# A two-layer diffusion backbone: second halves of the first scale and shift by high and low parts, constant products first, head reordered

## Chip, cores and metric

The kernel runs on one core of one Trainium2 chip. The metric is device time in microseconds (us), the median of several runs. TensorE multiplies matrices; VectorE (DVE), ScalarE (ACT) and GpSimd (POOL) work elementwise; SyncE (SP) issues most loads. Each engine executes its own instructions strictly in the order in which they were written for it, and semaphores make it wait for others.

## What is computed

Two layers over 256 latent tokens and 256 context tokens of width 1024, float32. Cut to what matters here, layer 0 begins so:

```python
mod_l = (silu(c) @ w_ada + b_ada)            # c: conditioning vector, w_ada: (1024, 6*1024)
mod_c = silu(c_ctx) @ w_ada + b_ada
sh1, sc1, g1, sh2, sc2, g2 = split(mod, 6)   # for latent and context
hl = xl * (1 + sc1_l) + sh1_l                # "h": the modulated input
hc = xc * (1 + sc1_c) + sh1_c
pl = hl @ w_in ; pc = hc @ w_in              # the wide input projection
# token mixers: Hyena long conv, attention, pooling; gates; output projection; layer norm; SwiGLU
# Hyena's filter: h = sin(freq*(feats@w1+b1)); h = sin(freq*(h@w2+b2)); h @ w3, times a window
```

So the first scale and shift (`sc1`, `sh1`) must be known before any token can be projected. They are two matrix-vector products: 1024x1024 weights each, against the two vectors `c` and `c_ctx`.

## The kernel before

A float32 product is made with the faster type `float32r` and three products: each operand is split into a high part (ScalarE, a copy to float32r, `L162`) and a low part (VectorE or GpSimd, the difference, `L159`), and `mm3` (`L169` to `L171`) sums high·high, high·low and low·high. Weights stream in blocks of 128x1024: `wfetch` loads `raw`, makes `whi` and `wlo` (or `wx`, for the first ones). A dense unit is 24 products (8 slices of the width, 3 each) with 512 columns (256 latent, 256 context tokens); its result is named `u`, `uv`, `ux` and so on.

The head of the program (`run`) does this:

- `ccol`, the two conditioning vectors, gets its silu (tanh on ScalarE, the rest on VectorE).
- `ada_raw(j, half)` loads half of the weights of shift (`j` 0) or scale (`j` 1): four tiles `adar` of 512 KB. "Half" is half of the 1024 output columns, so the first half modulates slices 0 to 3 of `h`, the second half slices 4 to 7. `ada_half` multiplies them in plain float32 with the two columns of `ccol` as the stationary operand (`L1220`, eight products of 512 columns), copies the row out (`adarow`, ScalarE), turns it into columns by four small transposes (`adat`, TensorE), and adds the bias (`mod`, VectorE).
- `first_h(x, h, half)` makes four slices of `h`, high part on ScalarE (`hh`), low part on VectorE and GpSimd (`hf`, `hl`).
- `early_half` runs the part of the first three dense units (`u`) that needs only the first half of `h`; the second half follows in the function `dense`.
- Hyena's filter is a background generator: a small product `L337`, a sine (`L309` to `L315`: VectorE brings the argument into range, ScalarE takes `Sin`), a small product `L343`, a second sine, a cast `hfh`, and then, per quarter, the weights `wfh` (`L398`) and the products `L406` and `L407`. `pump()` lets it take its next step, so the calls of `pump` set where its instructions stand.
- The rows of `silu` (`csg`, `L1179`) are for later adaLN weights.

Nothing decides at run time. The tile framework orders the instructions of each engine when the program is built; `with self.tc.high_priority(n)` moves a block ahead of others in that order. Tiles of one tag rotate through a fixed number of buffers (`bufs`), and a new one waits until the old one's readers are done. After the head, TensorE runs one dense unit after another to the end.

Of the kernel before, what the change touches and what calls it, by code (L numbers as in the profile page):

```python
# [11 lines left out]
F32R = mybir.dt.float32r  # L12
I32 = mybir.dt.int32
AF = mybir.ActivationFunctionType
ALU = mybir.AluOpType
# [3 lines left out]
P = 128  # L19
D = 1024  # L20
KT = D // P
# [31 lines left out]
V_CW, V_CB, V_BADA, V_QG, V_KG, V_HYD = 40, 112, 136, 184, 185, 186  # L53
NV = 194
# [11 lines left out]
class Kernel:  # L66
# [868 lines left out]
    def fold(self, g, b, sc, sh):  # L935

        nc = self.nc
        f = self.small([P, 2, KT], "fold", tag="fold", bufs=8)
        nc.vector.tensor_tensor(out=f[:, 0], in0=g, in1=sc, op=ALU.mult)
        nc.vector.tensor_tensor(out=f[:, 1], in0=b, in1=sc, op=ALU.mult)  # L940
        nc.vector.tensor_tensor(out=f[:, 1], in0=f[:, 1], in1=sh, op=ALU.add)
        return f[:, 0], f[:, 1]

    def scaled(self, g, b):
        f = self.small([P, 2, KT], "alp", tag="fold", bufs=8)
# [179 lines left out]
    def run(self):  # L1125
        nc = self.nc
        cc = self.const([P, KT, 2], "ccol")
        nc.scalar.dma_start(out=cc, in_=self.c_col)
        self.vecs = self.const([P, DEPTH, NV + 6], "vecs")
        self.ones = self.const([P, P], "ones")  # L1130
        nc.vector.memset(self.ones, 1.0 / D)
        self.ident = self.const([P, P], "ident")
        make_identity(nc, self.ident)
        self.mod = [[self.const([P, 2, KT], f"mod{l}{j}") for j in range(6)] for l in range(DEPTH)]
        th = self.const([P, KT, 2], "ccolt")
        nc.scalar.activation(th, cc, AF.Tanh, scale=0.5)
        nc.vector.tensor_scalar(out=th, in0=th, scalar1=0.5, scalar2=0.5, op0=ALU.mult, op1=ALU.add)
        nc.vector.tensor_tensor(out=cc, in0=cc, in1=th, op=ALU.mult)
        x = self.big(F32, [P, KT, 512], name="x")
        h = self.pair(512, "h")  # L1140
        self.start_filters(0)
        self.start(itertools.chain(self.filter_hidden(0), self.filter_chain(0)))
        raws = [self.ada_raw(1, 0), self.ada_raw(0, 0)]
        nc.scalar.dma_start(out=self.vecs[:, :, :NV], in_=self.vecs_d)
        nc.sync.dma_start(out=x[:, 0:4], in_=self.x_t[:, 0:4])
        for j, raw in zip((1, 0), raws):
            with self.tc.high_priority(200):
                self.ada_half(cc, j, 0, raw)
            self.pump()
        self.first_h(x, h, 0)  # L1150

        wx = self.big(F32R, [P, 2, 2, D], name="wx")
        for i in range(2):
            self.wfetch((wx[:, i, 0], wx[:, i, 1]))
        raws = self.ada_raw(1, 1)
        self.wfetch(None, nc.gpsimd)
        self.early = [(self.wq.popleft(), self.mm(name="u")) for _ in range(3)]
        self.early_half(h, *self.early[0], 0)
        for j in (1, 0):
            with self.tc.high_priority(1000):  # L1160
                self.ada_half(cc, j, 1, raws)
            if j:
                raws = self.ada_raw(0, 1)
                for k in (4, 6):
                    nc.sync.dma_start(out=x[:, k : k + 2], in_=self.x_t[:, k : k + 2])
                for w, o in self.early[1:]:
                    self.early_half(h, w, o, 0)
# [37 lines left out]
    def ada_raw(self, j, half):  # L1205

        raws = []
        for kp in range(4):
            raw = self.t4(shape=[P, 2, 512], name="adar")
            self.nc.sync.dma_start(out=raw, in_=self.ada0[j, half * 4 + kp])  # L1210
            raws.append(raw)
        return raws

    def ada_half(self, cc, j, half, raws):

        nc = self.nc
        o = self.aux(name="adar")
        for kp in range(4):
            for k in range(2):
                nc.tensor.matmul(o[:2], lhsT=cc[:, 2 * kp + k], rhs=raws[kp][:, k], start=kp + k == 0, stop=kp + k == 4)  # L1220
        row = self.t2(name="adarow")
        nc.scalar.activation(row[:2], o[:2], AF.Copy)
        tp = self.aux([P, 4, 2], name="adat")
        for m in range(4):
            nc.tensor.transpose(tp[:, m], row[:2, m * P : (m + 1) * P], self.ident[:2, :2])
        c = 4 * half
        for s in range(2):
            nc.vector.scalar_tensor_tensor(out=self.mod[0][j][:, s, c : c + 4], in0=tp[:, :, s], scalar=float(j),
                                           in1=self.v(0, V_BADA + 8 * j + c, 4), op0=ALU.add, op1=ALU.add)

# [126 lines left out]
```

## Time and profile before

| | us |
|---|---|
| runs | 1717.17, 1719.15, 1722.42; median 1719.15 |
| the profiled execution | 1716.89 |
| its span, first to last instruction | 1715.1 |
| TensorE busy in the span | 1662.9 (97%) |
| VectorE busy | 1218.8 (71%) |
| ScalarE busy | 709.1 (41%) |
| GpSimd busy | 224.6 (13%) |
| first matmul of the scale and shift | 6.38 |
| first matmul of the fourth dense unit (`uv`) | 57.86 |

Times in the trace count from the span's start; 1.8 us of the execution lie around the span. A share of busy time is an average over stages: this change touches the first 60 us alone, and what it is worth is read from who waits for whom there.

### The profile page before, as it was taken

The page shows a single profiled execution, that of the slowest core. Times are in us where ns is not written, and L with a number is a line of the kernel's source. Part 1 is how long each engine was busy: PE and PEld are TensorE (multiplying, and loading weights), DVE is VectorE, ACT ScalarE, POOL GpSimd, SP SyncE. Part 2 cuts the span into 40 slices and gives each one's busy share as a digit, 9 for nine tenths or more (in the row PEclk, how much of TensorE's full clock was granted, in tenths as well). Part 3 has the DMA queues.
Part 4 walks back from the last instruction along what each step waited for, and adds up shares of the span by engine and source line. Part 5 has one row for each costly group of instructions (what it writes and reads, how often), then busy time and mean ns, then how long its engine had stood idle before and what let it go on. Part 6 is the DMA issues. An engine that isn't in the chain of part 4 may idle for free.

```text
span 1715.1 us, 25592 instructions
## 1 busy us (share of the span) xinstructions
PE 1662.9 (97%) x9926; PEld 1448.2 (84%) x9926; DVE 1218.8 (71%) x2124; ACT 709.1 (41%) x1130; POOL 224.6 (13%) x232
## 2 busy tenths in 40 slices
PE   8999999999999999999999999998899999999996
PEld 1888888888888888988888877898899999989996
DVE  3777778755677775788876566498866696796655
ACT  3533432534454433542222222264435564564442
POOL 1134541000210000000000011124510210000000
PEclk9999999999999999999999999999999999999998
DMA  8422222553422344226666654244336525645552
GB/s 322 149 87 87 62 87 75 153 158 125 135 74 90 113 160 130 98 91 196 193 201 191 210 177 148 62 149 131 115 108 194 172 89 161 196 140 190 182 186 89
DMA packets 68898, 243.35 MB, mean 142 GB/s; under 512 B 8166, under 2 KB 8744, under 8 KB 68520
## 3 DMA queue, kind: packets, MB, share of 16 engines
q1 hardware_dynamic: 67192, 236.78, 43.3%
q0 software_dynamic: 1168, 4.72, 0.9%
q8 instruction: 78, 1.28, 0.3%
q14 instruction: 44, 0.36, 0.1%
q10 hardware_dynamic: 416, 0.21, 0.1%
HBM read 238.01 MB, written 1.05 MB: 139 GB/s over the span
## 4 chain that ended last, share of the span: by engine, by line
PE 82%; DVE 11%; ACT 2%; issue 2%; POOL 1%; DMA 1%; ACTq 0%; DVEq 0%; POOLq 0%
PE f L169 6%; PE f L171 6%; PE f L170 6%; PE b L169 4%; PE g L169 4%; PE g L171 4%; PE g L170 4%; PE b L171 4%; PE b L170 4%; PE w L169 4%; PE w L171 4%; PE w L170 4%; DVE wlo L159 2%; PE ux L169 2%; PE ux L171 2%
## 5 line engine op out<-in xcount | busy, mean ns | idle before, releaser
L162 ACT ACTIVATE whi<-raw 128x1024 fp32r<-128x1024 f32 x322 | 340.7, 1059 | 710.9 <-issue 210.4
L159 DVE TENSOR_TENSOR wlo<-raw,whi 128x1024 fp32r<-128x1024 f32 x311 | 397.8, 1280 | 216.0 <-ACT whi L162 214.0
L190 DVE SCALAR_TENSOR_TENSOR junk<-ada,silu 128x1024 bf16<-128x1024 f32 x128 | 158.7, 1241 | 38.6 <-DMA ada<-adat 38.0
L169 PE MATMUL f<-h2h,whi 128*128 128x512 f32 (+1 forms) x320 | 125.1, 391 | 0.1
L170 PE MATMUL f<-h2l,whi 128*128 128x512 f32 (+1 forms) x320 | 124.5, 389 | 0.0
L171 PE MATMUL f<-h2h,wlo 128*128 128x512 f32 (+1 forms) x320 | 124.5, 389 | 0.0
L169 PE MATMUL w<-a,whi 128*128 128x256 f32 (+1 forms) x284 | 90.3, 318 | 0.0
L169 PE MATMUL f<-h,whi 128*128 128x256 f32 x312 | 88.4, 283 | 1.9 <-DVE fraw L930 1.9
L170 PE MATMUL w<-a,whi 128*128 128x256 f32 (+1 forms) x284 | 89.2, 314 | 0.0
L171 PE MATMUL w<-a,wlo 128*128 128x256 f32 (+1 forms) x284 | 89.2, 314 | 0.0
L171 PE MATMUL f<-h,wlo 128*128 128x256 f32 x312 | 87.6, 281 | 0.6 <-DVE wlo L159 0.6
L170 PE MATMUL f<-h,whi 128*128 128x256 f32 x312 | 88.1, 283 | 0.0
L169 PE MATMUL g<-hh,whi 128*128 128x512 f32 x192 | 75.6, 394 | 0.0
L171 PE MATMUL g<-hh,wlo 128*128 128x512 f32 x192 | 75.4, 392 | 0.0
L170 PE MATMUL g<-hl,whi 128*128 128x512 f32 x192 | 75.3, 392 | 0.0
L169 PEld LDWEIGHTS f<-h2h,whi 128*128 128x128 f32 x320 | 60.0, 188 | 14.1 <-DVE sg L973 0.9
L171 PEld LDWEIGHTS f<-h2h,wlo 128*128 128x128 f32 x320 | 60.1, 188 | 13.6
L170 PEld LDWEIGHTS f<-h2l,whi 128*128 128x128 f32 x320 | 60.1, 188 | 13.1
L169 PEld LDWEIGHTS f<-h,whi 128*128 128x128 f32 x312 | 58.4, 187 | 2.4 <-issue 2.3
L171 PEld LDWEIGHTS f<-h,wlo 128*128 128x128 f32 x312 | 59.3, 190 | 0.8 <-DVE wlo L159 0.8
L170 PEld LDWEIGHTS f<-h,whi 128*128 128x128 f32 x312 | 58.6, 188 | 0.0
L169 PEld LDWEIGHTS w<-a,whi 128*128 128x128 f32 x284 | 53.4, 188 | 4.1 <-issue 0.2
(474 smaller groups left out, 4802.0 us busy)
## 6 DMA issues: line engine op xcount, KB each, us to landing
raw<-wst SPq DMA_DIRECT2D x336, 512.0 KB, 3.5
ada<-adat SPq DMA_DIRECT2D x80, 512.0 KB, 3.8
adar<-ada SPq DMA_DIRECT2D x16, 512.0 KB, 10.2
qsw<-q POOLq DMA_DIRECT2D x16, 128.0 KB, 5.2
x<-x_t POOLq DMA_DIRECT2D x1, 2048.0 KB, 9.6
x<-x_t SPq DMA_DIRECT2D x1, 1024.0 KB, 10.6
x<-x_t SPq DMA_DIRECT2D x2, 512.0 KB, 10.2
silu<-c_row SPq DMA_DIRECT2D x2, 512.0 KB, 7.5
```

The costliest lines, as they stand in the source:

```text
L159: (eng or self.nc.vector).tensor_tensor(out=lo, in0=src, in1=hi.bitcast(F32), op=ALU.subtract)
L162: self.nc.scalar.activation(hi, src, AF.Copy)
L169: t.matmul(out, lhsT=ah, rhs=bh, start=start, stop=False)
L170: t.matmul(out, lhsT=ah, rhs=bl, start=False, stop=False)
L171: t.matmul(out, lhsT=al, rhs=bh, start=False, stop=stop)
L190: nc.vector.scalar_tensor_tensor(out=junk, in0=raw, scalar=1.0, in1=self.silu[:, s], op0=ALU.mult, op1=ALU.mult, accum_out=mod[:, s, m : m ...
```

## The change

1. Twelve products of the constant tile `ones` with itself are written ahead of all other work of TensorE; nobody reads their result.
2. The first halves of scale and shift are multiplied as before, but both groups directly one after the other (class `Ada`, `passes`), and each is turned into columns afterwards (`columns`).
3. The second halves (`half == 1`) are no longer plain float32: `ccol` is split into four columns `ccolp` (two high, two low), each of the eight weight tiles is split into high (`ahi`, ScalarE, in buffers of the tags `whi` and `wlo`) and low (`alo`, VectorE, in two buffers of the tag `big`), and 16 products per group give four rows, which the product with `fold4` turns into columns and adds up.
4. The head is reordered: the scale's second half comes ahead of the first half of `h`; the tables of the long convolution (`start_filters`, `dft_tables`) come later; the third weight's low part is made by VectorE and no longer by GpSimd; the filter's steps come at other calls of `pump`.
5. `fold` and `alp` rotate through 7 buffers where there were 8; `ccolt` is a tile of the tag `t2`.

```diff
-        f = self.small([P, 2, KT], "fold", tag="fold", bufs=8)
+        f = self.small([P, 2, KT], "fold", tag="fold", bufs=7)
...
+        o = self.aux(name="warm")
+        for _ in range(12):
+            nc.tensor.matmul(o[:, :P], lhsT=self.ones, rhs=self.ones, start=True, stop=True)
...
+        cp = self.sb.tile([P, KT, 4], F32R, tag="ccolp", name="ccolp", bufs=1)
+        self.split(cp[:, :, 0:2], cp[:, :, 2:4], cc)
+        self.fold4 = self.vecs[:4, 0, NV : NV + 2]
+        nc.vector.tensor_tensor(out=self.fold4, in0=self.ident[:4, 0:2], in1=self.ident[:4, 2:4], op=ALU.add)
...
-        self.start_filters(0)
         self.start(itertools.chain(self.filter_hidden(0), self.filter_chain(0)))
-        raws = [self.ada_raw(1, 0), self.ada_raw(0, 0)]
+        first = [Ada(self, cc, 1, 0), Ada(self, cc, 0, 0)]
...
-        for j, raw in zip((1, 0), raws):
-            with self.tc.high_priority(200):
-                self.ada_half(cc, j, 0, raw)
-            self.pump()
+        with self.tc.high_priority(1000):
+            first[0].passes(0, 4)
+            first[1].passes(0, 4)
+            first[0].columns()
+        self.pump()
+        scale = Ada(self, cc, 1, 1)
+        with self.tc.high_priority(1000):
+            scale.passes(0, 1)
+            first[1].columns()
+
+        wx = self.big(F32R, [P, 2, 2, D], name="wx")
+        self.wfetch((wx[:, 0, 0], wx[:, 0, 1]))
+        with self.tc.high_priority(1000):
+            scale.passes(1, 4)
+            scale.columns()
         self.first_h(x, h, 0)
...
+        self.wfetch((wx[:, 1, 0], wx[:, 1, 1]))
+        shift = Ada(self, cc, 0, 1)
+        self.early = [(self.wq.popleft(), self.mm(name="u")) for _ in range(2)]
+        for w, o in self.early:
+            self.early_half(h, w, o, 0)
+        with self.tc.high_priority(500):
+            shift.passes(0, 4)
+            shift.columns()
+        for k in (4, 6):
+            nc.sync.dma_start(out=x[:, k : k + 2], in_=self.x_t[:, k : k + 2])
+        with self.tc.high_priority(1000):
+            self.wfetch()
+        self.early.append((self.wq.popleft(), self.mm(name="u")))
+        self.early_half(h, *self.early[2], 0)
+        self.start_filters(0)
         self.dft_tables(0)
-        with self.tc.high_priority(50):
+        with self.tc.high_priority(1000):
             self.first_h(x, h, 1)
+        self.pump()
...
+class Ada:
...
+    def passes(self, a, b):
+        k = self.k
+        self.o = self.o or k.aux(name="adar")
+        for kp in range(a, b):
+            ws = [self.raws[kp]]
+            if self.parts:
+                tag = ("whi", "wlo")[kp % 2]
+                ws = [k.sb.tile([P, 2, 512], F32R, tag=tag, name=k.nm("ahi"), bufs=3), self.los[:, kp]]
+                k.split(*ws, self.raws[kp])
+            for i in range(2):
+                for m, w in enumerate(ws):
+                    k.nc.tensor.matmul(self.o[: self.n], lhsT=self.cc[:, 2 * kp + i], rhs=w[:, i],
+                                       start=kp + i + m == 0, stop=kp + i == 4 and m == len(ws) - 1)
```

The order that this gives differs from that of before in the head alone. Three places of it follow. The first is ScalarE's queue around the filter's first sine (`hf1h`; `adarow` are the rows of scale and shift, `ahi` the high parts of the scale's second half). Before:

```order
L1222 ACTIVATE adarow_123<-adar_114 2x512
L315 ACT_TABLE_LOAD
L315 ACTIVATE hf1h_134<-sa_135 64x256
L1222 ACTIVATE adarow_154<-adar_145 2x512
L1195 ACTIVATE hh_88<-x_87,mod_71,mod_72 128x256 x7
L315 ACTIVATE hf2h_165<-sa_166 128x256
```

The same place after the change:

```order
L1260 ACTIVATE adarow_147<-adar_129 2x512
L162 ACTIVATE ahi_179<-adar_169 128x1024
L162 ACTIVATE ahi_200<-adar_171 128x1024
L315 ACT_TABLE_LOAD
L315 ACTIVATE hf1h_158<-sa_159 64x256
L1260 ACTIVATE adarow_186<-adar_138 2x512
L162 ACTIVATE ahi_207<-adar_173 128x1024
L162 ACTIVATE ahi_214<-adar_175 128x1024
L162 ACTIVATE wx_195<-raw_196 128x1024
```

Two high parts stand ahead of the sine now; behind it stand the shift's row (`adarow_186`), the other two high parts and the first weight. The second sine (`hf2h`) has left this place.

The second place is VectorE's queue around the argument of that second sine (`sa_166`, `sa_402`). Before, it stands between the shift's first half (`mod_71`) and the first half of `h`:

```order
L1228 SCALAR_TENSOR_TENSOR mod_71<-adat_156,vecs 128x4 x2
L309 TENSOR_SCALAR sa_166<-hf_25_163,hfs_92 128x256
L310 TENSOR_SCALAR sn_167<-sa_166 128x256
L311 TENSOR_SCALAR sn_167<-sn_167 128x256
L313 SCALAR_TENSOR_TENSOR sa_166<-sn_167,sa_166 128x256 x3
L314 TENSOR_SCALAR sa_166<-sa_166 128x256
L1197 TENSOR_SCALAR hf_180<-x_87,mod_72,mod_71 128x256
```

After the change it stands at the end of the second half of `h` (`hl_106` is its last low part; `hyb` is a table, `wlo_424` a weight):

```order
L159 TENSOR_TENSOR hl_106<-hf_392,hh_105 128x256
L309 TENSOR_SCALAR sa_402<-hf_77_399,hfs_107 128x256
L159 TENSOR_TENSOR hyb_360<-dftraw_363,hyb_360 128x512
L310 TENSOR_SCALAR sn_403<-sa_402 128x256
L159 TENSOR_TENSOR wlo_424<-raw_421,whi_423 128x1024
L311 TENSOR_SCALAR sn_403<-sn_403 128x256
L313 SCALAR_TENSOR_TENSOR sa_402<-sn_403,sa_402 128x256 x3
L314 TENSOR_SCALAR sa_402<-sa_402 128x256
L1198 SCALAR_TENSOR_TENSOR silu<-csg_430,silu 128x512
```

It moved from before the first low part of `h` to behind the last one.

The third place is TensorE's queue at the filter's first quarter (`hf` with `wfh` and `hfh`). Before, it stands behind the dense unit `uv`:

```order
L169 MATMUL uv_451<-hh_88,whi_358 128x512
L170 MATMUL uv_451<-hl_89,whi_358 128x512
L171 MATMUL uv_451<-hh_88,wlo_359 128x512
L406 MATMUL hf_91_476<-wfh_438,hfh_176 128x256
L407 MATMUL hf_91_476<-wfl_439,hfh_176 128x256
```

After the change two of its eight products stand ahead of `uv`, behind the last of the units `u`:

```order
L170 MATMUL u_347<-hl_106,whi_343 128x512
L171 MATMUL u_347<-hh_105,wlo_344 128x512
L406 MATMUL hf_103_535<-wfh_497,hfh_412 128x256
L406 MATMUL hf_104_541<-wfh_497,hfh_412 128x256
L169 MATMUL uv_510<-hh_105,whi_417 128x512
```

They moved ahead by one dense unit, and with them the wait for `wfh` and `hfh`.

## Rows read from the trace of the kernel before

**Rows 1.** The page, busy time: us, share of the span, instructions.

```profile
PE 1662.9 (97%) x9926; PEld 1448.2 (84%) x9926; DVE 1218.8 (71%) x2124; ACT 709.1 (41%) x1130; POOL 224.6 (13%) x232
```

**Rows 2.** Timeline of TensorE: start, length, instruction, count, [idle before <- releaser].

```profile
6.38 8.96 PE L1220 MATMUL adar<-adar,ccol 128*2 128x512 f32 x16 [6.38 <-DVE ccol L1138]
16.11 0.38 PE L1225 MATMUL adat<-ident,adarow 2*128 2x2 f32 x4 [0.77 <-ACT adarow L1222]
16.41 0.64 PE L337 MATMUL hf<-feats,hfs 33*64 33x256 f32 x2
16.99 7.03 PE L1220 MATMUL adar<-adar,ccol 128*2 128x512 f32 x16
...
34.73 7.03 PE L1220 MATMUL adar<-adar,ccol 128*2 128x512 f32 x16
...
42.81 0.41 PE L1225 MATMUL adat<-ident,adarow 2*128 2x2 f32 x4
...
57.86 0.40 PE L169 MATMUL uv<-hh,whi 128*128 128x512 f32 x1
58.09 0.39 PE L170 MATMUL uv<-hl,whi 128*128 128x512 f32 x1
```

**Rows 3.** Timeline of VectorE.

```profile
17.10 0.54 DVE L309 TENSOR_SCALAR sa<-hf,hfs 64x256 f32<-64x256 f32 x1 [0.34 <-PE hf L337]
...
18.30 1.32 DVE L313 SCALAR_TENSOR_TENSOR sa<-sn,sa 64x256 f32<-64x256 f32 x3
19.66 0.29 DVE L314 TENSOR_SCALAR sa<-sa 64x256 f32<-64x256 f32 x1
...
25.76 0.54 DVE L309 TENSOR_SCALAR sa<-hf,hfs 128x256 f32<-128x256 f32 x1 [0.40 <-PE hf L343]
...
34.45 1.75 DVE L159 TENSOR_TENSOR wx<-raw,wx 128x1024 fp32r<-128x1024 f32 x1
...
36.26 3.22 DVE L159 TENSOR_TENSOR wx<-raw,wx 128x1024 fp32r<-128x1024 f32 x1
43.25 0.23 DVE L1228 SCALAR_TENSOR_TENSOR mod<-adat,vecs 128x4 f32<-128x4 f32 x2 [3.77 <-PE adat L1225]
...
49.85 2.35 DVE L159 TENSOR_TENSOR wlo<-raw,whi 128x1024 fp32r<-128x1024 f32 x2
```

**Rows 4.** Timeline of ScalarE.

```profile
20.05 1.28 ACT L315 ACT_TABLE_LOAD   x1 [4.08 <-DVE sa L314]
21.34 0.42 ACT L315 ACTIVATE hf1h<-sa 64x256 f32<-64x256 f32 x1
24.05 0.59 ACT L1222 ACTIVATE adarow<-adar 2x512 f32<-2x512 f32 x1 [2.29 <-PE adar L1220]
...
29.97 1.99 ACT L162 ACTIVATE wx<-raw 128x1024 fp32r<-128x1024 f32 x2
...
49.94 1.28 ACT L1179 ACT_TABLE_LOAD   x1
...
55.97 0.62 ACT L398 ACTIVATE wfh<-wf 128x512 fp32r<-128x512 f32 x1
```

**Rows 5.** The page, loads: KB each, median us from issue to landing.

```profile
raw<-wst SPq DMA_DIRECT2D x336, 512.0 KB, 3.5
```

**Rows 6.** Busy time of each engine by stretch (us, count); then granted clock, DMA share, GB/s.

```profile
43.45:48.76 5.31, 5.31 (x24) 4.32 (x23) 5.31 (x14) 5.31 (x10) 2.61 (x4) 1.00 0.88 323
49.94:56.59 6.65, 6.65 (x30) 5.37 (x29) 6.55 (x9) 5.55 (x8) 0.00 (x0) 1.00 0.61 201
```

**Rows 7.** The same view, around two idle times of TensorE later in the span.

```profile
740.20:742.20 2.00, 0.00 (x0) 0.00 (x0) 1.93 (x7) 0.62 (x2) 0.00 (x0) 1.00 0.31 63
742.20:746.00 3.80, 3.77 (x32) 3.77 (x33) 3.80 (x11) 3.62 (x8) 0.00 (x0) 1.00 0.26 105
...
1167.70:1172.80 5.10, 0.08 (x2) 0.07 (x1) 5.10 (x8) 1.52 (x3) 3.81 (x3) 0.81 0.10 41
1172.80:1177.70 4.90, 4.90 (x23) 4.90 (x24) 4.25 (x6) 0.00 (x0) 2.77 (x2) 0.50 0.37 107
```

More of the change, by code (lines that the diff above doesn't have):

```diff
@@ L944, in scaled @@
     def scaled(self, g, b):
-        f = self.small([P, 2, KT], "alp", tag="fold", bufs=8)
+        f = self.small([P, 2, KT], "alp", tag="fold", bufs=7)
         self.nc.vector.tensor_scalar_mul(f[:, 0], g, ALPHA)
@@ L1134, in run @@
         self.mod = [[self.const([P, 2, KT], f"mod{l}{j}") for j in range(6)] for l in range(DEPTH)]
-        th = self.const([P, KT, 2], "ccolt")
+        th = self.t2(name="ccolt")[:, : 2 * KT].rearrange("p (k s) -> p k s", s=2)
         nc.scalar.activation(th, cc, AF.Tanh, scale=0.5)
@@ L1138, in run @@
         nc.vector.tensor_tensor(out=cc, in0=cc, in1=th, op=ALU.mult)
+        cp = self.sb.tile([P, KT, 4], F32R, tag="ccolp", name="ccolp", bufs=1)
+        self.split(cp[:, :, 0:2], cp[:, :, 2:4], cc)
+        self.fold4 = self.vecs[:4, 0, NV : NV + 2]
+        nc.vector.tensor_tensor(out=self.fold4, in0=self.ident[:4, 0:2], in1=self.ident[:4, 2:4], op=ALU.add)
+        cc = (cc, cp)
         x = self.big(F32, [P, KT, 512], name="x")
         h = self.pair(512, "h")
-        self.start_filters(0)
@@ L1152, in run @@
[L1152 to L1167, printed above, removed]
+        with self.tc.high_priority(1000):
+            first[0].passes(0, 4)
+            first[1].passes(0, 4)
+            first[0].columns()
@@ L1203, in early_half, with __init__, columns @@
             self.mm3(o, (w[0][:, ks], w[1][:, ks]), h[k], k == 0, k == KT - 1)
-    def ada_raw(self, j, half):
-        raws = []
-        for kp in range(4):
[L1209 to L1223, printed above, removed]
-        for m in range(4):
-            nc.tensor.transpose(tp[:, m], row[:2, m * P : (m + 1) * P], self.ident[:2, :2])
-        c = 4 * half
+class Ada:
+    def __init__(self, k, cc, j, half):
+        self.k, self.j, self.half = k, j, half
+        self.parts = half == 1
+        self.n = 4 if self.parts else 2
+        self.cc = cc[half]
+        self.raws = []
+        for kp in range(4):
+            raw = k.t4(shape=[P, 2, 512], name="adar")
+            k.nc.sync.dma_start(out=raw, in_=k.ada0[j, half * 4 + kp])
+            self.raws.append(raw)
+        if self.parts:
+            self.los = k.big(F32R, [P, 4, 2, 512], name="alo")
+        self.o = None
+    def passes(self, a, b):
[3 more added lines that the diff above has]
+            ws = [self.raws[kp]]
+            if self.parts:
+                tag = ("whi", "wlo")[kp % 2]
[5 more added lines that the diff above has]
+                                       start=kp + i + m == 0, stop=kp + i == 4 and m == len(ws) - 1)
+    def columns(self):
+        k, j, n = self.k, self.j, self.n
+        nc = k.nc
+        row = k.t2(name="adarow")
+        nc.scalar.activation(row[:n], self.o[:n], AF.Copy)
+        tp = k.aux([P, 4, 2], name="adat")
+        for m in range(4):
+            if n == 2:
+                nc.tensor.transpose(tp[:, m], row[:2, m * P : (m + 1) * P], k.ident[:2, :2])
+            else:
+                nc.tensor.matmul(tp[:, m], lhsT=row[:n, m * P : (m + 1) * P], rhs=k.fold4[:n], start=True, stop=True)
+        c = 4 * self.half
@@ L1227, in ada_half @@
         for s in range(2):
-            nc.vector.scalar_tensor_tensor(out=self.mod[0][j][:, s, c : c + 4], in0=tp[:, :, s], scalar=float(j),
-                                           in1=self.v(0, V_BADA + 8 * j + c, 4), op0=ALU.add, op1=ALU.add)
+            nc.vector.scalar_tensor_tensor(out=k.mod[0][j][:, s, c : c + 4], in0=tp[:, :, s], scalar=float(j),
+                                           in1=k.v(0, V_BADA + 8 * j + c, 4), op0=ALU.add, op1=ALU.add)
 def _constants():
```

## The prediction

> **What bounds the kernel now.** The page's first line comes first: TensorE is busy for 1662.9 of 1715.1 us [rows 1]. So a delay in the head passes to the end unless TensorE has slack later, and the question is when the fourth dense unit, `uv`, starts. TensorE's timeline gives that: the four groups of scale and shift stand almost without a gap from 6.38 on, and `uv` starts at 57.86 [rows 2]. The first group takes 8.96, each other 7.03, so the start of the first runs at a lower rate and costs 1.93. VectorE's and ScalarE's timelines then show how much room these two have: VectorE still waited 3.77 for TensorE at 43.25 [rows 3], and ScalarE 4.08 at its first table load [rows 4]. In before they wait for TensorE. The change gives both more to do, so I follow both in their new order.
>
> Loads are not the bound: a weight block lands 3.5 after its issue [rows 5]. The head's new order holds SyncE's table load until the scale's low parts are read, at about 32 by the steps below, and with it the weight blocks behind it; those are the blocks of `uv` and later, which are wanted from about 47 on.
>
> **The first groups.** Twelve products of 128 columns: a group is eight products of 512 columns and takes 7.03, so 0.88 a product and 0.22 for a quarter of it; at half clock 0.44. Eleven stand ahead of the first group and would end near 6, before `ccol` is there at 6.38. Then both groups run at 7.03: 6.38 + 14.06 = 20.4, where before it was 24.0. The transposes (0.38) and the filter's small product `L337` (0.64) follow, with one leftover constant product: `L337` starts at about 21.0 and TensorE is done at 21.6. If a constant product cost as much as a 512-column one, the first group would be 4 later; if they don't raise the clock, 1.9 later; those are the bounds.
>
> **The first new wait.** The first second-half group needs VectorE's first low part `alo`. It stands behind four of the five lines of the sine's argument. Before, the argument started 0.69 after `L337` (16.41 to 17.10) and ended at 19.95, 2.85 in all [rows 3]. So it starts at 21.7, and the low part (2.35 / 2 = 1.17) ends at about 25.4: TensorE idles from 21.6 to 25.4. The argument ends at 25.7; ScalarE, in its fixed order, then does the table load 1.28, the sine 0.42, the shift's row 0.59 and two high parts 1.99 [rows 4], and ends at 30.0. The first two high parts are done by then, since they don't wait for the sine.
>
> The table load is where a page of the Trainium skill says otherwise. In the trace a load of 1.28 at 20.05 is followed by the sine at 21.34, at once [rows 4]. The Trainium skill, "ScalarE: Activation LUTs", § What ACT_TABLE_LOAD costs, gives about 1283 ns for the load and a drain of about 1380 ns besides. With that drain on both loads of the chain the time would be 2.8 longer; the rows show no such gap, and I leave it out.
>
> **VectorE becomes the bound.** From 29.0, when the third high part is there, VectorE has three low parts (3 x 1.17, to 32.5) and then the first half of `h`. That costs what the second half cost before: between 43.45 and 48.76 VectorE is busy for all 5.31 [rows 6]. The scale's columns come about 0.4 late, so it ends at 38.2. Six low parts follow, four of the shift and two of weights: 7.0, to 45.2. TensorE then has the two last products (0.23 each, from `uv`'s starts at 57.86 and 58.09 [rows 2]), and copy, transposes and bias take 1.5, as from 41.76, the end of the last group, to 43.25. The last shift is there at 47.2, before at 43.25: 4 later, though the four groups end in less TensorE time.
>
> A `float32r` product with four columns as the stationary operand is in no row. The near row is 0.23 for 512 columns; the far one is 0.88, a plain float32 product. At the far end a group is 16 x 0.65 = 10 longer; I take the near one, since the moving operand is of the same size and type. A low part beside GpSimd's work took 1.75 and 3.22 in place of 1.17 [rows 3]. Two low parts here stand beside GpSimd's `hl`, so between 0 and 1.1 comes on top; I take 0.6. `fold4`, the split of `ccol`, and the smaller rotation of `fold` are tiny or early, and hidden by the first groups.
>
> **The second new wait.** The second half of `h` runs 5.31 from 47.4 on, with one weight's low part between: to 53.9. Only then comes the argument of the second sine, with the table `hyb` (half a low part, 0.6) and another weight (1.17) in between: 2.85 + 1.77, to 58.5. Then ScalarE: `hf2h` 0.42 (as the first sine), then the table load, the four `csg`, two evacuations and `wfh`. Before, this stretch, 49.94 to 56.59, held 5.55 of ScalarE work [rows 6], and `hfh` (taken as another 0.42) has joined it. So `wfh` is ready at 58.5 + 0.42 + 5.55 + 0.42 = 64.9.
>
> TensorE is out of work before that: the last part of `h` is there about 0.5 behind VectorE's, at 54.4, and 20 products of 0.23 end at 59.0. Then two `L406` stand ahead of `uv` and wait until 64.9: 5.9 of idle time. Behind them the whole of `uv` is queued, though its weights are ready. Before, `wfh` was ready (56.59) before its place in the queue came. With 0.6 for the two products `uv` starts at 65.5; since these two no longer stand behind it, the program is 65.5 - 57.86 - 0.6 = 7.0 later.
>
> **The clock after an idle place.** Two places show both ends [rows 7]. Behind an idle 2.0 (740.2 to 742.2) the granted clock stays 1.00. Behind an idle 5.1 with little work in it (1167.7 to 1172.8) it is 0.50 for the next 4.9, which is 1.2 GHz in place of 2.4, and loses 2.45. The second new wait is 5.9, so I take 2.4 (0 to 3.4). The first, 3.8, lies between the two; TensorE is not the bound behind it, so I take 0.3 (0 to 2).
>
> **The sum.** 7.0 + 0.6 + 2.4 + 0.3 = 10.3. The order behind the head is the same as before, so nothing else changes. On the profiled execution of 1716.89 that gives 1727.2, on the median of 1719.15 it gives 1729.5: I say 1728.
>
> **Rivals.** *Faster:* the splits hide and TensorE's own work sets the end. It would be 21.6 + 2 x (3.7 + 0.4) + 72 x 0.23 = 46.4, about 47 with its last wait, 10.9 before 57.86: 1706. The Trainium skill, "Perfetto Trace Analysis", § Identifying the Most-Contended Engine, would send one to that: the change relieves the busiest engine. Against it: from 21.7 VectorE alone has thirteen low parts (15.2), two halves of `h` (10.6), two arguments (5.7) and `hyb` (0.6): 32.1, to 53.8, without any wait. For a gain the second wait with its clock (8.3) has to vanish, and a low part has to cost 0.15 less, that is about 1.0. The trace has nothing for a cheaper one. Chance 0.10.
>
> *No change:* the delay comes back later, 1716 to 1724. TensorE is idle for 52.2 in all [rows 1]; were it waiting for loads there, a later start would cost nothing. Against it: in the two idle places of [rows 7] VectorE is busy for 1.93 of 2.00 and all of 5.10, and the load share is small, so they move with the rest. Also here: part of the second wait is gone because the sine's argument gets through earlier. Chance 0.14.
>
> *Worse:* the half clock of the first idle lasts through the sparse stretch behind it, and comes again after the second. Then the products between 25 and 47 on the path cost twice (about 1.2), and `uv`'s 24 products 5.6 in place of 2.4; with the upper end of GpSimd's share, 10.3 + 1.2 + 3.2 + 0.5 = 15: 1732 on the profiled execution, 1734 on the median. For it: after the first wait TensorE has only some two thirds of its time filled. Chance 0.16.
>
> *Forecast:* both waits, +6 to +13. Chance 0.60.
>
> **How the numbers follow.** A measurement of this kernel tells about 0.3% (5.2) from no change. Slower takes the forecast and the worse case, 0.76; same 0.14; faster 0.10. The range leaves out the faster case and a tail on each side: from 1719, where the forecast's waits are nearly gone, to 1735, the worse case's end.
>
> **What would show it.** In the changed profile: TensorE idle at about 21.6 to 25.4, released by VectorE's `alo`, and at about 59 to 65, released by ScalarE's `wfh`; a table load at about 25.7; the last shift at 47; `uv` at 65.5, its clock at 0.50. If the first pair of groups doesn't take 14.06, the constant products fail; if second-half products take far over 0.23, or a low part more or less than 1.17, VectorE's sum is off. If `uv` starts before 60, or starts late but the unit after the filter is back at its old time, the forecast is wrong.

## The result, and the profile after

The changed kernel takes 1733.48 us (median of 5 runs, 1729.47 to 1741.46) against 1717.97 (5 runs, 1717.17 to 1722.42): a ratio of 1.0083, 95% interval 1.0068 to 1.0098. It is slower, as forecast, and inside the range; the sum was 1727 to 1729.5 and so 4 to 6 short. The profiled execution took 1733.48 with a span of 1731.7, 16.6 more than before.

The page's line of busy time after shows TensorE busy 11.9 longer, and the span 16.6 longer [rows 1]:

```profile
PE 1674.8 (97%) x9958; PEld 1457.3 (84%) x9958; DVE 1227.7 (71%) x2135; ACT 716.3 (41%) x1139; POOL 225.8 (13%) x231
```

A good mark for what the head costs is the first product of the fifth dense unit, `ux`: everything that the change moves lies ahead of it. TensorE's timeline has it at 65.83 before and at 79.01 after, 13.2 later:

```profile
65.83 0.50 PE L169 MATMUL ux<-hh,whi 128*128 128x512 f32 x1
```

```profile
79.01 0.50 PE L169 MATMUL ux<-hh,whi 128*128 128x512 f32 x1
```

The rest of TensorE's head after (start, length, instruction, idle time ahead and its releaser) answers to [rows 2]:

```profile
1.06 4.47 PE L1135 MATMUL warm<-ones 128*128 128x128 f32 x22 [1.06 <-DVE ones L1131]
7.88 15.59 PE L1253 MATMUL adar<-adar,ccol 128*2 128x512 f32 x32 [2.34 <-DVE ccol L1142]
...
24.15 0.64 PE L337 MATMUL hf<-feats,hfs 33*64 33x256 f32 x2
28.55 0.52 PE L1253 MATMUL adar<-alo,ccolp 128*4 128x512 f32 x1 [3.43 <-DVE alo L159]
28.86 0.63 PE L1253 MATMUL adar<-ahi,ccolp 128*4 128x512 f32 x1
29.29 0.63 PE L1253 MATMUL adar<-alo,ccolp 128*4 128x512 f32 x1
...
43.24 0.40 PE L1253 MATMUL adar<-ahi,ccolp 128*4 128x512 f32 x1
43.48 0.40 PE L1253 MATMUL adar<-alo,ccolp 128*4 128x512 f32 x1
...
51.32 1.05 PE L1266 MATMUL adat<-vecs,adarow 4*128 4x2 f32 x8
...
69.67 0.80 PE L406 MATMUL hf<-wfh,hfh 128*128 128x256 f32 x2 [5.13 <-ACT wfh L398]
70.33 0.79 PE L169 MATMUL uv<-hh,whi 128*128 128x512 f32 x1
```

Both forecast idle places are there: 3.43 for VectorE's first low part, and 5.13 for ScalarE's `wfh`. The products of the second halves follow one another at 0.24 where the clock is full (43.24 to 43.48) and at 0.43 where it is half (28.86 to 29.29). VectorE and ScalarE after answer to [rows 3, 4]:

```profile
7.29 0.17 DVE L946 TENSOR_SCALAR alp<-vecs 128x8 f32<-128x8 f32 x1 [6.29 <-DMA vecs<-vecs]
...
27.28 1.21 DVE L159 TENSOR_TENSOR alo<-adar,ahi 128x1024 fp32r<-128x1024 f32 x1
...
52.40 0.23 DVE L1269 SCALAR_TENSOR_TENSOR mod<-adat,vecs 128x4 f32<-128x4 f32 x2 [2.90 <-PE adat L1266]
...
63.11 0.29 DVE L314 TENSOR_SCALAR sa<-sa 128x256 f32<-128x256 f32 x1
...
69.53 0.74 DVE L542 SCALAR_TENSOR_TENSOR vv<-u,vecs,vv 128x510 f32<-128x510 f32 x1
```

```profile
28.80 1.28 ACT L315 ACT_TABLE_LOAD   x1 [7.72 <-DVE sa L314]
30.09 0.42 ACT L315 ACTIVATE hf1h<-sa 64x256 f32<-64x256 f32 x1
...
63.50 0.42 ACT L315 ACTIVATE hf2h<-sa 128x256 f32<-128x256 f32 x1 [5.38 <-DVE sa L314]
63.93 1.28 ACT L1197 ACT_TABLE_LOAD   x1
65.23 0.63 ACT L1197 ACTIVATE csg<-silu 128x512 f32<-128x512 f32 x1
...
69.00 0.62 ACT L398 ACTIVATE wfh<-wf 128x512 fp32r<-128x512 f32 x1
```

The reader is to see one thing more. `uv` starts at 70.33, and VectorE's `L542` on the first unit's `vv` ends at 69.53 + 0.74 = 70.27. The accumulators of the dense units (tag `mm`) have three buffers, so `uv` takes that of the first `u`, and `L542` is the last reader of that one. The second wait has two ends that come almost together: `wfh` at 69.62 and this evacuation at 70.27. The view of waits names only the first.

Busy time and granted clock by stretch after, as in [rows 6, 7] (length; busy time and count of TensorE, its weight loads, VectorE, ScalarE, GpSimd; clock, DMA share, GB/s): the two first groups, the sparse stretch behind the first wait, the second wait, and what follows it.

```profile
7.88:23.47 15.59, 15.59 (x33) 2.88 (x34) 0.23 (x2) 2.89 (x4) 0.00 (x0) 0.89 1.02 412
23.80:49.40 25.60, 20.02 (x71) 9.30 (x70) 21.02 (x36) 15.22 (x21) 3.86 (x4) 0.80 0.59 219
64.54:69.67 5.13, 0.00 (x1) 0.00 (x1) 3.72 (x7) 5.12 (x10) 0.00 (x0) 1.00 0.05 14
69.67:73.03 3.36, 3.36 (x8) 2.65 (x9) 3.36 (x5) 1.56 (x2) 0.71 (x1) 0.50 0.03 5
```

### The profile page after: what moved, and what is told of

Read it like the earlier page. It is cut to its first block, busy times and chain, and to the rows that moved or that the text cites. A ratio compares the mean times of both kernels' runs of the same rounds, so it can differ in the third digit from the quotient of the medians.

```text
span 1731.7 us, 25685 instructions
## 1 busy us (share of the span) xinstructions
PE 1674.8 (97%) x9958; PEld 1457.3 (84%) x9958; DVE 1227.7 (71%) x2135; ACT 716.3 (41%) x1139; POOL 225.8 (13%) x231
## 3 DMA queue, kind: packets, MB, share of 16 engines
q8 instruction: 78, 1.28, 0.3%
HBM read 238.01 MB, written 1.05 MB: 138 GB/s over the span
## 4 chain that ended last, share of the span: by engine, by line
PE 79%; DVE 12%; ACT 2%; issue 2%; POOL 1%; DMA 1%; ACTq 0%; DVEq 0%; POOLq 0%
PE f L171 6%; PE f L169 6%; PE f L170 6%; PE b L169 4%; PE b L170 4%; PE b L171 4%; PE g L169 4%; PE g L171 4%; PE g L170 4%; PE w L169 4%; PE w L171 3%; PE w L170 3%; DVE wlo L159 2%; PE ux L169 2%; PE ux L171 2%
## 6 DMA issues: line engine op xcount, KB each, us to landing
x<-x_t SPq DMA_DIRECT2D x2, 512.0 KB, 10.2
```

## Experiments

Two theories stood at the start. **Theory 1** is the prediction's: VectorE's low parts and the two waits cost the time, and each wait can be taken away by itself. **Theory 2** is that the new order alone costs it, with or without parts. The table has all kernels; `ux` is the mark from above, "head" its distance from 65.83. "Both end" is the end of the two first groups where they stand one behind the other, and "behind" is `ux` less that end. Times are compared with the kernel before on the same chip (medians 1717.9 to 1719.5), as a ratio with its 95% interval. The times of one kernel spread by up to 12 us, likely in part for a reason that lies behind the head (last section), so the head is read from `ux`, in one profiled execution each. The end of the first groups itself differs by 4.7 between these executions, with the landing of `vecs` and with the rate at which the first products run; what an edit behind them is worth is therefore read from "behind".

| kernel | first group | both end | `uv` | `ux` | head | behind | median us | ratio |
| --- | --- | --- | --- | --- | --- | --- | --- | --- |
| the change | 7.88 | 23.47 | 70.33 | 79.01 | +13.2 | 55.5 | 1733.48 | 1.0083 (1.0068 to 1.0098) |
| plain | 6.30 | 20.19 | 67.49 | 76.52 | +10.7 | 56.3 | 1729.90 | 1.0073 (1.0060 to 1.0086) |
| hf3_late | 7.80 | 23.06 | 72.27 | 79.36 | +13.5 | 56.3 | 1739.61 | 1.0125 (1.0111 to 1.0138) |
| sine1_later | 7.84 | 21.73 | 67.57 | 76.57 | +10.7 | 54.8 | 1734.16 | 1.0092 (1.0078 to 1.0106) |
| const18 | 7.56 | 21.45 | 69.10 | 78.47 | +12.6 | 57.0 | 1736.27 | 1.0101 (1.0084 to 1.0118) |
| sine2_early | 7.75 | 24.59 | 71.23 | 79.22 | +13.4 | 54.6 | 1733.80 | 1.0084 (1.0067 to 1.0100) |
| plain_sine2_early | 7.61 | 21.50 | 62.05 | 70.03 | +4.2 | 48.5 | 1724.68 | 1.0029 (1.0018 to 1.0040) |
| before_parts | 7.26 | - | 67.03 | 75.02 | +9.2 | - | 1727.49 | 1.0045 (1.0030 to 1.0059) |
| before_const | 7.17 | - | 62.29 | 70.26 | +4.4 | - | 1723.14 | 1.0022 (1.0012 to 1.0033) |
| hi_only | 8.03 | 24.89 | 65.72 | 73.20 | +7.4 | 48.3 | 1724.53 | 1.0026 (1.0015 to 1.0036) |
| plain_cols | 6.99 | 20.88 | 56.60 | 64.58 | -1.3 | 43.7 | 1722.61 | 1.0013 (1.0001 to 1.0025) |
| const_fix | 7.35 | - | 56.89 | 64.86 | -1.0 | - | 1716.90 | 0.9982 (0.9972 to 0.9992) |
| vecs_later | 5.62 | - | 55.16 | 63.14 | -2.7 | - | 1716.02 | 0.9982 (0.9973 to 0.9991) |

The two first groups in plain, sine2_early, plain_sine2_early and hi_only, in this order:

```profile
6.30 13.89 PE L1253 MATMUL adar<-adar,ccol 128*2 128x512 f32 x32 [0.18 <-DVE ccol L1142]
7.75 16.84 PE L1253 MATMUL adar<-adar,ccol 128*2 128x512 f32 x32 [1.63 <-DVE ccol L1142]
7.61 13.89 PE L1253 MATMUL adar<-adar,ccol 128*2 128x512 f32 x32 [1.78 <-DVE ccol L1142]
8.03 16.86 PE L1253 MATMUL adar<-adar,ccol 128*2 128x512 f32 x32 [1.91 <-DVE ccol L1142]
```

**plain: the parts taken out.**

```diff
-        self.parts = half == 1
+        self.parts = False
-        self.cc = cc[half]
+        self.cc = cc[0]
```

> The changed kernel with the second halves in plain float32 again, two columns and no parts; order and constant products as in the change. If VectorE's low parts and the two waits are the cost, the eight low parts (8 x 1.2) leave VectorE, the first idle time (3.4) goes, the shift's columns come at about 44 instead of 52.4, and wfh comes at about 60: uv at 60 to 61, and the time is 1718 to 1723. If the new order alone costs the time, with or without the parts, uv still starts at 68 or later and the time stays at 1729 or more.

The first alternative did not come out, and the second nearly did (67.49 in place of 68 for `uv`, 1729.90 for the time): the head gets 2.5 better, not 8 or more, and even that is not the parts. The first groups ended 3.3 earlier here, and behind them `ux` came no sooner (56.3, and 55.5 in the change). So the new order alone costs as much as the whole change, as theory 2 says. The first wait is gone, but another stands in its place (2.57, for the row of the shift's first half, which ScalarE makes behind the sine's table load), and the second wait stays at 3.45. TensorE's timeline of this kernel names both of its releasers, one behind the other:

```profile
66.83 0.51 PE L406 MATMUL hf<-wfh,hfh 128*128 128x256 f32 x2 [3.45 <-ACT wfh L398]
67.49 0.64 PE L169 MATMUL uv<-hh,whi 128*128 128x512 f32 x1 [0.15 <-DVE vv L542]
```

**hf3_late: the filter's quarter one step later.** The move also changes a part of what is computed behind the head, so that only the head is read here; and the filter's eight products, 2.4 long before (63.39 to 65.83), no longer stand ahead of its `ux`, so that its head reads that much too small.

```diff
             self.first_h(x, h, 1)
-        self.pump()
```

> The changed kernel without the call of pump behind the second half of h, so that the filter's first quarter (wfh, L406) stands one dense unit later. If the wait for wfh costs 5.1 of idle time and 1.7 of half clock, uv starts at about 64.6 instead of 70.3 and the time falls by 6 to 7, to 1726 or 1727. If TensorE would have to wait for something else there anyway (a weight's low part, an evacuation), the idle time moves and the time falls by less than 2, 1732.

`L406` no longer stands ahead of `uv`, and the wait did not go; it grew to 8.40. The view names `wfh` again, although no product that reads it stands ahead:

```profile
72.27 0.77 PE L169 MATMUL uv<-hh,whi 128*128 128x512 f32 x1 [8.40 <-ACT wfh L398]
```

VectorE's timeline shows what `uv` waits for. The same step of the filter holds the second sine, which now stands behind the silu rows, with a table load of its own, and still ahead of the evacuation:

```profile
67.28 0.29 DVE L314 TENSOR_SCALAR sa<-sa 128x256 f32<-128x256 f32 x1
70.14 0.75 DVE L540 SCALAR_TENSOR_TENSOR vv<-u,vecs,vv 128x510 f32<-128x510 f32 x1 [2.57 <-ACT vv L538]
...
71.38 0.75 DVE L542 SCALAR_TENSOR_TENSOR vv<-u,vecs,vv 128x510 f32<-128x510 f32 x1
```

71.38 + 0.75 = 72.13, and `uv` starts at 72.27. So of the second wait the prediction knew one half. What holds both halves back is the second sine among the last work of VectorE and ScalarE.

**sine1_later: the first sine behind the scale's columns.**

```diff
             first[0].columns()
-        self.pump()
...
             scale.columns()
+        self.pump()
         self.first_h(x, h, 0)
```

> The changed kernel with the filter's first step called behind the scale's columns, so that no sine stands ahead of the scale's low parts. If VectorE's queue is the bound from 24 to 63 and the first wait comes from the sine's argument ahead of the low part, the idle time of 3.4 at 25 goes, VectorE regains about 3 of its 4.3 idle between 24 and 50, and uv comes 2 to 4 earlier; the wait for wfh stays at about 5: time 1729 to 1732. If the first wait is hidden by later slack, nothing moves: uv at 70, 1733.

The idle time of 3.4 at 25 goes, `uv` comes 2.8 earlier, and the wait for `wfh` stays (4.09), as expected. But 1.7 of the 2.8 were there when the first groups ended, so that some 1.0 is left for the first wait. The median does not show it.

**const18: more constant products.**

```diff
-        for _ in range(12):
+        for _ in range(18):
```

> The changed kernel with 18 constant products instead of 12. In its trace TensorE idles for 2.34 between the constant products and the first group, and the clock falls back to 0.50 from 8.18 to 11.59, so the first two groups took 15.59 instead of 14.06. If that idle time is what loses the clock, the six more products fill most of it, the groups take about 14.1 and everything behind comes 1.5 earlier: uv at about 69, time about 1732. If the clock falls there for another reason, the groups stay at 15.6.

Not a test of its question: only 11 of the 18 stand ahead of the first group in the order, the other seven behind the two groups. The gap stayed at 1.90, and yet the clock did not fall and the groups took 13.89. So the 1.7 that the groups lost in the changed kernel's profile (gap of 2.34) is no fixed cost. The gap does not tell either whether it is paid: behind 1.73 in sine1_later and 1.78 in plain_sine2_early the groups took 13.89 as well, but behind 1.68 in hf3_late, 1.63 in sine2_early and 1.91 in hi_only they took 15.26, 16.84 and 16.86. (The seven constant products behind the groups take 1.3 of const18's 57.0.)

**sine2_early: the second sine ahead of the first half of `h` again.**

```diff
             scale.columns()
+        self.pump()
         self.first_h(x, h, 0)
...
             self.first_h(x, h, 1)
-        self.pump()
```

> The changed kernel with the second call of pump ahead of the first half of h again, as in the kernel before, so that the second sine and its argument stand there and not between the second half of h and the silu rows. If the late sine holds back ScalarE's table load, and with it both wfh and the evacuation vv that frees the buffer of uv, the table load starts right behind hyb, the idle time ahead of uv (5.1) and the half clock behind it go, the argument's 2.9 on VectorE comes 20 us earlier instead, and uv starts at about 67: time 1727 to 1730. If VectorE's sum of work alone sets uv, it still starts at 70 and the time stays at 1733.

The second wait is gone (no idle time ahead of `uv`), and little is gained: the shift's last columns come at 57.70 in place of 52.40 (1.1 of it from the first groups), and `ux` 0.9 sooner behind the first groups. With the parts, VectorE has no room for the argument where it now stands. By stretch, the two idle places at 26.2 and 42.2 with what lies around them:

```profile
26.24:37.60 11.36, 7.30 (x20) 2.23 (x20) 8.27 (x14) 6.03 (x9) 0.00 (x0) 0.55 0.63 250
41.00:51.20 10.20, 5.07 (x12) 2.37 (x13) 10.02 (x17) 7.57 (x10) 3.04 (x1) 0.50 0.07 11
```

VectorE is busy for 10.02 of 10.20 while TensorE has half of its time to do, at 0.50. The rival in this expectation holds, as far as this run goes: with the parts, VectorE's sum sets `uv`, wherever the sine stands. hi_only (below) tests it.

**plain_sine2_early: both taken back.** The edits of plain and sine2_early together.

> The same move in the kernel with plain float32 second halves (plain started uv at 67.5 after an idle time of 3.4). If the late sine is the larger cost and the parts the smaller, uv starts at 62 to 63 without a wait and the time is 1722 to 1725. If the order of the four groups (both first groups ahead of all columns) is what costs, uv stays at 66 or later and the time at 1728 or more.

As expected: 62.05, 1724.68. Taking back the parts alone gives 2.5 of the head, the sine alone nothing, both 9.0. Counted behind the first groups it is clearer: 55.5 in the change, 56.3 without the parts, 54.6 with the sine early, 48.5 with both. They are two limits side by side, and each hides behind the other.

**hi_only: the low parts alone.** sine2_early, but a weight tile gives only its high part:

```diff
-                ws = [k.sb.tile([P, 2, 512], F32R, tag=tag, name=k.nm("ahi"), bufs=3), self.los[:, kp]]
-                k.split(*ws, self.raws[kp])
+                ws = [k.sb.tile([P, 2, 512], F32R, tag=tag, name=k.nm("ahi"), bufs=3)]
+                k.nc.scalar.activation(ws[0], self.raws[kp], AF.Copy)
```

> The kernel sine2_early without the eight low parts of the second halves' weights: the low rows of the weights are left out of scale and shift, all else (high parts, four columns, fold4, order) stays. If VectorE's sum of work sets uv in the version with parts, the 9.6 that leave it bring uv from 71.2 to 61 to 63, as in plain_sine2_early (62.05), and the time to 1722 to 1726. If ScalarE's eight high parts, or the tables and columns around the parts, cost as much, uv stays at 66 or later and the time at 1728 or more.

The time is as expected for VectorE as the bound (1724.53, 9.3 below sine2_early); `uv` in the profile is between the two (65.72), 5.5 below sine2_early. Of the 3.7 that it lies above plain_sine2_early, 3.4 were there when the first groups ended. Behind them the two kernels need the same (48.3 and 48.5), so the eight low parts account for all that the parts cost here, 6.3 of 54.6; the eight high parts on ScalarE, which stayed, do not show. Nor does it show in this balance that TensorE idles for 4.21 at 27 and then runs at 0.50 for all of a stretch that is three quarters filled:

```profile
32.00:48.00 16.00, 12.13 (x31) 6.45 (x31) 11.34 (x26) 13.17 (x20) 3.11 (x4) 0.50 0.27 93
```

**before_parts: the parts alone, in the order of before** (with the tables started later, since the parts need their buffers).

```diff
-                self.ada_half(cc, j, 1, raws)
+                self.ada_parts(cp, j, 1, raws)
```

> The kernel before with one part of the change alone: the second halves by high and low parts (with the tables of the convolution started later, since the parts need their buffers); order, sines and first halves as before, no constant products. If VectorE's eight low parts are a cost by themselves, they and the two weights' parts fill VectorE to about 49, the shift's columns come 5 to 6 later than 43.25, and uv starts at 61 to 63: time 1721 to 1724. If parts are hidden and TensorE's saving of 14.06 - 7.4 counts, uv starts at 52 to 56 and the time is 1711 to 1716.

The direction is right and the size too small: +9.2, not 3 to 5. Of this 1.4 were there when the second group started (18.43, before 16.99). The low parts end at 51 rather than 49, because the two weights' parts ahead of them take 5.06 beside GpSimd's, and TensorE runs at half clock for 13.7 after an idle time of 5.35.

```profile
35.85 5.06 DVE L159 TENSOR_TENSOR wx<-raw,wx 128x1024 fp32r<-128x1024 f32 x2
40.84 8.02 DVE L159 TENSOR_TENSOR alo<-adar,ahi 128x1024 fp32r<-128x1024 f32 x7
```

**before_const: the constant products alone.**

```diff
+        o = self.aux(name="warm")
+        for _ in range(12):
+            nc.tensor.matmul(o[:, :P], lhsT=self.ones, rhs=self.ones, start=True, stop=True)
```

> The kernel before with one part of the change alone: the twelve constant products ahead of all. If they raise the clock before the first group, it takes 7.0 instead of 8.96, TensorE stays busy, and the time is 1.5 to 2 less, about 1716. If the idle time between them and the first group loses the clock again, or the gain is spent in a later wait, the time stays within 0.5 of 1718.

Neither: the first group does take 7.03 in place of 8.96 (its length, [rows 2]), and the kernel is slower. The edit changed the order as well. One product with the weight's low part stands ahead of the scale's columns now; it waits, and the last group runs at half clock:

```profile
35.10 0.80 PE L171 MATMUL u<-hh,wx 128*128 128x512 f32 x1 [2.90 <-DVE wx L159]
36.69 0.58 PE L1229 MATMUL adat<-ident,adarow 2*128 2x2 f32 x4
37.20 8.97 PE L1224 MATMUL adar<-adar,ccol 128*2 128x512 f32 x16
```

**plain_cols: the columns of both first halves ahead of the first sine,** on top of plain_sine2_early.

```diff
             first[0].columns()
+            first[1].columns()
         scale = Ada(self, cc, 1, 1)
...
             scale.passes(0, 1)
-            first[1].columns()
```

> The kernel plain_sine2_early with the columns of both first halves written ahead of the filter's first step, so that the row of the shift's first half no longer waits behind the sine's table load. In plain_sine2_early TensorE idled for 2.57 there (25.5 to 28.07) and ran at half clock for 3.4 behind it. If that is what still separates it from the kernel before, uv comes 3 to 4 earlier, at 58 to 59, and the time is 1719 to 1722. If the delay sits in the loads or in VectorE, uv stays at 61 or later and the time at 1724.

The head gains more than expected (5.4) and is ahead of the kernel before by 1.3. The time is 1722.61, just above what was expected for it: the head's gain is lost behind the head. VectorE's `fold` that stands at 446.82 and 824.26 before comes at 446.50 and 825.74 here, and the span ends 2.9 later. About 1.4 of the loss falls at 743, where the granted clock is 0.50 for 3.4 and the kernel before, as profiled, lost nothing.

**const_fix: constant products without the wait.** before_const, with the first half of an early unit in two passes, first all products with the weight's high part, then those with its low part:

```diff
     def early_half(self, h, w, o, half):
+        for part in ((0, 1) if half == 0 else (2,)):
...
+                elif part == 0:
+                    self.nc.tensor.matmul(o, lhsT=w[0][:, ks], rhs=h[k][0], start=k == 0, stop=False)
+                    self.nc.tensor.matmul(o, lhsT=w[0][:, ks], rhs=h[k][1], start=False, stop=False)
+                else:
+                    self.nc.tensor.matmul(o, lhsT=w[1][:, ks], rhs=h[k][0], start=False, stop=False)
```

> The kernel before with the twelve constant products, and with the first half of each early unit written so that its products with the weight's low part (L171) come last. In before_const one such product stood ahead of the scale's columns, waited 2.9 for its low part, and the last group ran at half clock behind that (8.97). If this wait is what ate the constants' gain, it goes: the last group takes 7.0, uv starts at 56 to 57.5 and the time is 1716 to 1718, at or below the kernel before. If the gain of 1.9 is lost elsewhere too, uv stays at 58 or later and the time at 1719 or more.

As expected, and faster than the kernel before. The last group takes 7.03 again, and `uv` starts 1.0 earlier although `ccol` came 1.0 later:

```profile
7.35 7.03 PE L1231 MATMUL adar<-adar,ccol 128*2 128x512 f32 x16 [1.47 <-DVE ccol L1142]
...
33.76 7.03 PE L1231 MATMUL adar<-adar,ccol 128*2 128x512 f32 x16
...
56.89 0.40 PE L169 MATMUL uv<-hh,whi 128*128 128x512 f32 x1
```

**vecs_later: `ccol` ahead of the wait for `vecs`,** on top of const_fix.

```diff
-        nc.scalar.dma_start(out=self.vecs[:, :, :NV], in_=self.vecs_d)
         nc.sync.dma_start(out=x[:, 0:4], in_=self.x_t[:, 0:4])
+        nc.sync.dma_start(out=self.vecs[:, :, :NV], in_=self.vecs_d)
```

> The kernel const_fix with the load of vecs (biases and other vectors) issued behind the first loads of x, so that VectorE makes ccol before it waits for vecs. In every trace so far ccol stands in VectorE's queue behind two small rows that wait for vecs, which landed between 5.7 and 7.3, and the first group started right after (6.3 to 8.0; 7.35 in const_fix). If this wait alone sets the first group's start, it starts when the constant products end, at about 5.9, and the time is 1 to 1.5 less than const_fix, 1715 to 1716. If the group's weights land no earlier than that, it still starts at 6.5 to 7.4 and the time stays at 1717.

The head does what was expected, and more: `ccol` is done at 3.40, the first group starts as the constant products end, and `ux` is 1.7 earlier than in const_fix.

```profile
5.62 7.03 PE L1231 MATMUL adar<-adar,ccol 128*2 128x512 f32 x16
```

```profile
3.23 0.17 DVE L1142 TENSOR_TENSOR ccol<-ccol,ccolt 128x16 f32<-128x16 f32 x1
```

The medians are 1716.02 and 1716.90, and the two ratios are the same within their intervals; the time does not separate the two. Both beat the kernel before by about 0.2%.

## Why the prediction was right

The direction holds, and both costs that the prediction named are real: the parts move work from TensorE, which had it, to VectorE, and the second sine now holds back the end of the head. before_parts shows that the parts cost 9.2 of the head by themselves, 7.8 without the later end of its first group, and hi_only that taking the low parts out of sine2_early gives back 6.3 behind the first groups and 9.3 of the time. What the prediction did not see is that either cost is enough. It strung both on one path, where the low parts make the shift late and the second wait follows; but without any parts (plain) the head is still 10.7 later, and the time (1.0073) is not separated from the change's (1.0083). That the sum came near is in part luck: steps that were too small and steps that were too large partly cancel.

The Trainium skill's "Perfetto Trace Analysis", § Identifying the Most-Contended Engine, has one optimize the engine with the highest occupancy first, which was TensorE [rows 1]; here relieving it failed, since the work went to an engine that TensorE then waits for.

Step by step, with the sizes:

- **First groups.** Forecast to end at 20.4, measured 23.47. They started at 7.88 in place of 6.38, because VectorE's queue has two rows ahead of it that wait for `vecs` (landed at 7.29, before at 5.79); and the clock fell for a time behind the gap, so that the groups took 15.59. Together 3.0. The constant products themselves were sized well (22 records in 4.47), but the forecast took the landing of `vecs` from one execution, and vecs_later shows that this wait sets the start. Nor did it allow for slow products at the start of the groups: with constant products ahead, the two groups took 13.89 in five of the nine kernels of this order and 15.26 to 16.86 in the other four.
- **First wait.** 3.8 forecast, 3.43 measured, for the low part behind the argument. Right.
- **Prices.** Second-half products 0.23 forecast, 0.24 measured at full clock; a low part 1.17, and 1.21 alone (27.28 in VectorE's rows). In both cases the near end of the bounds was the right one. The transposes with `fold4` are eight records and 1.05 long, not 0.4: a term of 0.6 that was missing. The term of 0.6 for GpSimd is about right: up to 60 no weight's low part took more than 1.22, and one `hl` took 0.95 (at 42.87) in place of 0.42.
- **Clock behind the first wait.** 0.3 forecast. The granted clock is 0.80 over the 25.6 from 23.8 on, which is 10.2 at 0.50 (twice 0.2 x 25.6); the second-half products took 0.43 each there, and ended (36.05) 1.7 behind VectorE's last low part of the scale (34.32). The reason given, that TensorE is not the bound there, is the step that failed: at half clock it is.
- **Shift's last columns.** 47.2 forecast, 52.40 measured: by estimate the 3.0 of the first groups, about 1 of the clock, 0.6 of `fold4`, and small rests.
- **Second wait.** 5.9 forecast, 5.13 measured, and `uv` 65.5 and 70.33: the difference of 4.8 comes from the 5.2 above. Its cause was half named: the evacuation of the first unit ends with `wfh`, so moving `L406` alone (hf3_late) frees nothing.
- **Clock behind it.** 2.4 forecast; 0.50 for 3.36 after it, which loses 1.7.

So the head was forecast at 10.3 and measured at 13.2. The remaining 3.4 of the profiled span lies behind the head. There the order did not change, but the sentence that nothing else changes failed; the last section has what is known of it.

The Trainium skill, "ScalarE: Activation LUTs", § What ACT_TABLE_LOAD costs, gives a drain besides the load. After the change the loads of 1.28 at 28.80 and 63.93 are followed by the next activation at 30.09 and 65.23, so no drain shows here either.

The rivals "faster" and "no change" did not come about: the delay of the head was carried through. The rival "worse" had its first half right, the half clock of the sparse stretch.

What stays open: why `vecs` lands between 5.7 and 7.4 in kernels that issue it at the same place in ScalarE's queue; why the first groups ran slowly in four executions; and the slower products behind the head (last section).

## What to carry to other kernels

Before work is taken off the busiest engine, add up what the receiving engine has to do between the same two events, and follow the queue of each engine to the next wait: here VectorE had slack only as long as TensorE's slow products covered it. When undoing one part of a change does nothing, undo two together before calling it harmless: two limits of nearly the same length hide each other, and a wait is put down to one of them. And look at the order of every engine after each edit, even one that only adds products: twelve constant products moved one dependent product ahead of a column step, and that cost more than they gave.

## What the runs showed of the hardware beyond that

An idle time of about 2.1 of TensorE may or may not cost the clock. At the same place in the program, between the same instructions, the kernel before idled for 2.00 and stayed at 1.00 [rows 7], and so did vecs_later; after the change the clock fell for the next 3.33. The changed kernel first, then vecs_later:

```profile
753.66:755.77 2.11, 0.01 (x2) 0.01 (x1) 2.04 (x7) 0.66 (x2) 0.00 (x0) 0.98 0.46 99
755.77:759.10 3.33, 3.33 (x15) 3.33 (x16) 3.33 (x9) 3.15 (x7) 0.00 (x0) 0.50 0.23 95
```

```profile
737.53:739.63 2.10, 0.00 (x1) 0.00 (x1) 2.03 (x7) 0.66 (x2) 0.00 (x0) 1.00 0.36 80
739.63:743.00 3.37, 3.37 (x28) 3.37 (x29) 3.37 (x9) 3.19 (x7) 0.00 (x0) 1.00 0.26 106
```

The same instructions behind this place come about 1.5 later where the clock fell, and the kernel before, as profiled, lost nothing there. At 1042.4 the changed kernel's clock fell to 0.50 for 3.4 although TensorE was busy for all of the 6.4 ahead of it; the kernel before stayed at 1.00 at that place, and this cost 1.6. This is likely one reason why the times of one kernel spread by more than the effects of the head that were looked for; it is not shown, since one execution of each kernel was profiled. The idle 2.0 at the full clock that the prediction read from one execution was one draw of several.

The 3.4 behind the head have a second part, which is no matter of the clock. Between two of VectorE's `fold` the kernel before and the changed kernel do the same work, with TensorE busy throughout and the clock at 1.00 in both, and the changed kernel takes 1.7 longer:

```profile
824.26:954.53 130.27, 130.27 (x568) 106.13 (x567) 91.10 (x141) 37.60 (x48) 0.00 (x0) 1.00 0.63 194
```

```profile
839.82:971.80 131.98, 131.98 (x567) 106.45 (x566) 91.20 (x141) 37.80 (x48) 0.00 (x0) 1.00 0.63 192
```

TensorE's products follow one another there at 0.233 on average in place of 0.230. All five kernels that have the low parts `alo` in the new order take 131.98 or 131.99 for this stretch; the other nine, before_parts with its low parts in the order of before among them, take 130.27 or 130.28. So this belongs to the kernel and not to the execution, and a change of the head can cost time far behind it. Other places give some time back (the three add up to 4.8, more than the 3.4). What makes the products slower is open.
